# Gates, projections up and mixtures by channel; the second block's input divided by its norm first; GpSimd's elementwise work on VectorE and ScalarE

## The chip, the core and the metric

The kernel runs on one core of one Trainium2 chip. The metric is the device time of one launch in microseconds (us). Three runs of the kernel before took 1385.99, 1386.69 and 1391.58 us; the median is 1386.69.

## The reference

512 tokens of width 1024 in fp32 pass through two blocks. `@` is a matrix product.

```
# first block
h     = rms_norm(x, norm_mix_g)
parts = h @ w_in                     # q, k, v of two attentions, small gates, g_a, g_b (1024 each)
out_a = fox_attention(...)  @ w_fox_up      # 8 heads, forget gates; 512 -> 1024
out_b = nsa_attention(...)  @ w_nsa_up      # 8 heads: compressed, selected, windowed keys; 512 -> 1024
mix   = sigmoid(g_a) * out_a + sigmoid(g_b) * out_b
x     = x + mix @ w_out
x     = x + hierarchical_moe(rms_norm(x, norm_ffn_g))     # 16 experts, 2 per token

# second block
u      = rmsnorm(x, g_pre)
proj   = u @ w_in_2                  # feat_a, z_a, c_q, c_kv, k_pe, z_b, gate logits (2048)
y_a    = rwkv7_branch(feat_a, z_a, ...)                   # ends with @ w_out_a
y_b    = mla_branch(c_q, c_kv, k_pe, z_b, ...)            # ends with @ w_out_b
gates  = sigmoid(gate_logits + b_gate)
merged = gates[:, :1024] * y_a + gates[:, 1024:] * y_b
out    = x + rmsnorm(merged @ w_o, g_post)
```

## The kernel before

Every large product is taken in three passes over split numbers (`mm3`, L118 to L120: high part by high part, low by high, high by low). A weight piece comes from DRAM as `raw`, ScalarE rounds it to `wh` (L109), VectorE subtracts to get `wl` (L112).

`linear_steps` (L128) gives a projection as a list of steps. 128 tokens are stationary and a piece of weight columns moves: with 256 columns a projection with 1024 rows of weight is 4 token tiles x 8 k x 3 matmuls of 128x256, and the result has tokens on the partitions. `Fill` (L291) puts such steps into TensorE's in-order stream between the products of the attention: `pull(t)` lets out steps worth t, each with a price of `3 * n / 2400` us, and `until(None)` lets out what is left. TensorE's stream is written out by hand in this way; on the other engines the scheduler orders the instructions.

First block, 0 to 550 us. q, k, v are projected, then come the heads of the two attentions with gates and projections up as fill (50 to 442 us). The norm's factor r of a token (`c.r`) is not in `hh`, `hl`; a gate applies it as the per-partition scale of its tanh (`tanh_to_dram`, and `gated` in `up`), since tokens are on the partitions there. The gates go to DRAM as `gd`, the gated first branch as `md` (`up`, L713). `twice`/`scaled` (L338) multiply q or k by their head norm on GpSimd, whose squares (L534) are on GpSimd too, and GpSimd adds the heads of the second attention into `ob` (L990). Then `merge` (L181) turns `ob` (L175), projects it with `w_nsa_up` in two halves of 512 columns, reads `gd` and `md`, forms `g = (g + 1) * product` (L201), `mix = mix + g` (L202), and turns `mix` on TensorE (`pt<-ident,mix`, L196) into `mh`, `ml` for `w_out`.

Experts run from 550 to 846 us. The second block begins at 846 us: `turned` (L214) adds the experts' part to x (L1454), multiplies by the gain (`xg`, L227), turns `xg` into `uh`, `ul` (L237), and projects the 416 columns of c_q, c_kv, k_pe. The squares are summed beside it (L241), r comes after the last product, `zc` is scaled by r on ScalarE (L2132), and `rr` is a row of r for each token, repeated over the partitions.

Then the second attention (`mla`, to 1012 us), the recurrence: `shifted` (L1584) projects 128 channels with tokens in the columns, multiplies by `rr` (L1590, VectorE) and shifts; `prepare` and `pairs` (1012 to 1150 us) make decays (`sw`, `C`), `GL`, `GR`, and `H` (L1689, GpSimd); an inversion (1150 to 1192 us), small products, a chain over 8 chunks (1230 to 1309 us). Gates of the second block are fill in these stages: `(product * r + bias)` on VectorE (L2176, L2218), tanh on ScalarE, `(tanh + 1) * product` (L2223). The same `merge` closes it, with `w_out_a` (1309 to 1339 us), then `w_o`, the last norm, and the sum with x.

Of the kernel before, what the change touches and what calls it, by code (L numbers as in the profile page):

```python
# [21 lines left out]
S = 512  # L22
# [18 lines left out]
class Ctx:  # L41
# [108 lines left out]
    def tanh_to_dram(self, pool, dst):  # L150

        def emit(i, ps):
            sg = pool.tile([128, 512], FT, name="sg", bufs=2)
            n = ps.shape[1]
            self.nc.scalar.activation(sg[:, :n], ps, AF.Tanh, scale=self.rh[:, i:i + 1])
            self.nc.sync.dma_start(dst(i), sg[:, :n])
        return emit

    def silu2_to_dram(self, pool, dst, scale=lambda i: 0.5):

        def emit(i, ps):
            sg = pool.tile([128, 512], FT, name="sg", bufs=2)
# [51 lines left out]
    def turned(self, x, get, gain, xgs, scr, hi, lo, steps, first=0):  # L214
# [5 lines left out]
        ms = self.sm.tile([128, NT], FT, name="ms")  # L220
        for _, f in loads[:first]:
            f()
        get(0)
        grow = gain()
        for i in range(NT):
            xg = xgs[i % 2]
            nc.vector.tensor_mul(xg, x[i], grow)  # L227
            if i == 0:
                for _, f in loads[first:]:
                    f()  # L230
            if i + 1 < NT:
                get(i + 1)
# [96 lines left out]
class Attention:  # L329
# [197 lines left out]
def _head_norm(c, z, w, name, scr_pool):  # L527
# [11 lines left out]
def first_mixer(c, I, at, hh, hl):  # L539
# [148 lines left out]
    gd = c.dram.tile([S, D], FT, name="gd")  # L688

    def gate(c0):  # L690
        return c.linear_steps(hh, hl, w_in, 3872 + c0, 256, c.tanh_to_dram(at, lambda i: gd[
            128 * i:128 * i + 128, c0:c0 + 256]))
    md = c.dram.tile([S, D], FT, name="md")
# [8 lines left out]
    def up(c0):  # L702

        m = []

        def gated(i, ps):
            if i % 2 == 0:
                m.append(at.tile([128, 2, 256], FT, name="sg", bufs=2))
            nc.scalar.activation(m[i // 2][:, i % 2], ps, AF.Tanh, scale=c.rh[:, i:i + 1])

        def emit(i, ps):
            v = m[i // 2][:, i % 2]
            nc.vector.scalar_tensor_tensor(v, v, 1.0, ps, op0=OP.add, op1=OP.mult)  # L713
            nc.scalar.dma_start(md[128 * i:128 * i + 128, c0:c0 + 256], v)
        return {f"a{c0}": c.linear_steps(hh, hl, w_in, 2848 + c0, 256, gated),
                f"u{c0}": c.linear_steps(lambda: ot, None, I["w_fox_up"][0], c0, 256, emit)}
# [11 lines left out]
    def second():  # L728
# [4 lines left out]
            ("gn_bias", I["gn_bias_2"], 0), ("g_q", I["g_q_2"], 0), ("g_kv", I["g_kv_2"], 0),  # L733
        ], "mm")
        late.append(trig(c, I, at))
    jobs |= {f"g{c0}": gate(c0) for c0 in range(0, D - 256, 256)}
# [38 lines left out]
    with tc.manual_schedule(engines={mybir.EngineType.PE}):  # L775
# [9 lines left out]
    mix = [at.tile([128, 2, D], FT, name="mix", tag=t, bufs=1) for t in ("t0", "t1")]
    mh, ml = (c.hp.tile([128, 8, S], FR, name=n, tag="f16", bufs=2) for n in ("mh", "ml"))
    ot = at.tile([128, 4, S], FR, name="obh", tag="kv", bufs=1), [
        at.tile([128, S], FR, name="obl", tag=t, bufs=n) for t, n in (("p", 3), ("p", 3), ("p", 3), ("cb", 2))]
    c.token_T(N.ob, *ot)
    c.merge(at, "q", 8, lambda: ot, I["w_nsa_up"][0], gd, md, mix, mh, ml)  # L790
# [55 lines left out]
class Nsa:  # L846
# [99 lines left out]
    def jobs(self, A, out):  # L946
# [14 lines left out]
        def job(h, b):  # L961
# [12 lines left out]
            def prep():  # L974
                if r == 0:
                    self.K[b] = A.keys(two["k"], c.cv["nsa_k"])
                if b == 0:
                    al[h] = at.tile([128, S], FT, name="cb", bufs=2)
                    nc.gpsimd.tensor_scalar(al[h], self.alibi, self.slopes[h], None, op0=OP.mult)
                return A.passes(self.Q[h], self.K[b]), lambda i: al[h][:, 384 - 128 * i:], False  # L980

            def done(pv, rb, ri):
                if r + g + b == 0:
                    self.ob = out()
                    nc.gpsimd.memset(self.ob, 0.0)
# [8 lines left out]
    def compressed(self, g):  # L994
# [14 lines left out]
        def softmax():  # L1009
# [12 lines left out]
            nc.gpsimd.tensor_sub(t, t, m[:, :, :, None].to_broadcast([128, NT, 4, 32]))  # L1022
# [15 lines left out]
        def values(i):  # L1038
# [8 lines left out]
            nc.gpsimd.tensor_add(o, o, tmp)  # L1047
# [26 lines left out]
def route(c, I, mh, ml, x2d, td, xp, keep):  # L1074
# [1228 lines left out]
```

## Time and profile before

| | |
|---|---|
| median of three runs | 1386.69 us |
| profiled execution | 1392.48 us, span of its instructions 1390.7 us |
| granted TensorE clock, mean | 0.960 of 2.4 GHz |
| busy TensorE / VectorE / ScalarE / GpSimd | 1277.1 / 974.8 / 755.6 / 259.3 us |
| chain of work that ended last | TensorE 65%, VectorE 17%, ScalarE 7%, DMA 6% |

A row of a timeline reads: start, length, engine, line, operation, out<-in, shapes, count, and in brackets how long the engine stood idle before it and what released it. Ends of matmuls are modelled, so the pitch of a stream is read from its starts. A group's row ends with busy time, mean length in ns of one, and the idle time before.

### The profile page before, as it was taken

Reading aid. Unit: us, or ns where it says so; the run is one execution under the profiler, and the core shown is the slowest. Engines: PE = TensorE matmul, PEld = TensorE weight load, DVE = VectorE, ACT = ScalarE, POOL = GpSimd, SP = SyncE. Lnnn points to the kernel's source line nnn. Section 1 sums busy time; section 2 is a strip of 40 time slices with the busy share of each in tenths; the row PEclk is TensorE's granted clock in tenths of the full one; section 3 lists DMA queues with packets and bytes.
Section 4 is the critical chain, followed back from the end, with each engine's and each line's share of the span. In section 5 each row is a group of like instructions: output and inputs, shape, how many; then the busy total and the mean of one; then the engine's idle time right before and its main releaser. Section 6 shows DMA issues by size and latency. Waiting matters only on the chain.

```text
span 1390.7 us, 24478 instructions
## 1 busy us (share of the span) xinstructions
PE 1277.1 (92%) x9240; PEld 1082.6 (78%) x9240; DVE 974.8 (70%) x2030; ACT 755.6 (54%) x1291; POOL 259.3 (19%) x226
## 2 busy tenths in 40 slices
PE   7999989988999995999999998999999999799997
PEld 6889978977898774677777776888977667788875
DVE  5664687666665646999999997767668769445555
ACT  5544565654544322788888885655557664233431
POOL 1111032211220002154444421000011012001000
PEclk9999989999999997999999998999999999799999
DMA  6332312222133497999999996541152334233543
GB/s 201 110 122 78 99 54 67 74 68 67 57 121 122 138 323 271 341 369 361 353 346 342 349 313 196 158 138 45 32 163 80 104 109 137 65 114 112 173 138 122
DMA packets 161294, 230.68 MB, mean 166 GB/s; under 512 B 21786, under 2 KB 97869, under 8 KB 161168
## 3 DMA queue, kind: packets, MB, share of 16 engines
q1 hardware_dynamic: 149760, 205.18, 45.1%
q0 software_dynamic: 6224, 18.62, 4.8%
q10 hardware_dynamic: 5184, 5.25, 1.1%
q8 instruction: 74, 1.21, 0.4%
q14 instruction: 52, 0.43, 0.1%
HBM read 200.63 MB, written 30.36 MB: 166 GB/s over the span
## 4 chain that ended last, share of the span: by engine, by line
PE 65%; DVE 17%; ACT 7%; DMA 6%; issue 4%; SPq 2%; POOL 0%; DVEq 0%; POOLq 0%; ACTq 0%
PE mm L118 14%; PE mm L119 14%; PE mm L120 14%; DMA raw<-in_w_in 3%; PE s L461 3%; DVE wl L112 3%; PE s L118 2%; PE s L119 2%; PE s L120 2%; PE pt L488 2%; ACT wh L109 1%; DVE itmp L1779 1%; PE x L118 1%; PE pt L1304 1%; DVE s L475 1%
## 5 line engine op out<-in xcount | busy, mean ns | idle before, releaser
L92 DVE TENSOR_TENSOR wl<-rawe,wh 128x1024 fp32r<-128x1024 f32 x192 | 224.7, 1218 | 23.7 <-ACT wh L90 23.6
L109 ACT ACTIVATE wh<-raw 128x512 fp32r<-128x512 f32 x214 | 131.7, 628 | 120.2 <-PE mm L120 42.5
L118 PE MATMUL mm<-wh,hh 128*128 128x256 f32 (+1 forms) x616 | 183.5, 298 | 12.5 <-ACT wh L109 3.3
L112 DVE TENSOR_TENSOR wl<-raw,wh 128x512 fp32r<-128x512 f32 x214 | 147.5, 702 | 63.7 <-ACT wh L109 58.5
L90 ACT ACTIVATE wh<-rawe 128x1024 fp32r<-128x1024 f32 x192 | 190.8, 1054 | 1.5 <-PE mm L120 1.5
L119 PE MATMUL mm<-wl,hh 128*128 128x256 f32 (+1 forms) x616 | 176.8, 287 | 0.1
L120 PE MATMUL mm<-wh,hl 128*128 128x256 f32 (+1 forms) x616 | 176.7, 287 | 0.2
L118 PEld LDWEIGHTS mm<-wh,hh 128*128 128x128 f32 (+1 forms) x616 | 119.1, 193 | 16.6 <-ACT wh L109 3.5
L119 PEld LDWEIGHTS mm<-wl,hh 128*128 128x128 f32 (+1 forms) x616 | 119.1, 193 | 1.8 <-DVE wl L112 0.4
L120 PEld LDWEIGHTS mm<-wh,hl 128*128 128x128 f32 (+1 forms) x616 | 118.9, 193 | 1.2 <-DVE hl L92 0.7
L1275 POOL DMA_INDIRECT xe<-td,slf x16 | 97.9, 6117 | 116.1 <-issue 73.4
L118 PE MATMUL mm<-wh,uh 128*128 128x256 f32 (+1 forms) x352 | 109.1, 310 | 5.2 <-DVE sg L2218 3.1
L479 ACT ACTIVATE p<-s,m 128x128 f32<-128x128 f32 (+3 forms) x128 | 67.3, 526 | 77.4 <-DVE m L475 54.6
L118 PE MATMUL mm<-wh,xh 128*96 128x512 f32 x256 | 103.5, 404 | 1.2 <-ACT xh L90 1.2
L119 PE MATMUL mm<-wl,uh 128*128 128x256 f32 (+1 forms) x352 | 103.7, 295 | 0.0
L120 PE MATMUL mm<-wh,ul 128*128 128x256 f32 (+1 forms) x352 | 103.4, 294 | 0.0
L120 PE MATMUL mm<-wh,xl 128*96 128x512 f32 x256 | 102.0, 398 | 0.4 <-DVE xl L92 0.4
L119 PE MATMUL mm<-wl,xh 128*96 128x512 f32 x256 | 101.1, 395 | 0.0
L492 DVE SCALAR_TENSOR_TENSOR pl<-pt,ph 128x384 f16<-128x384 f32 (+1 forms) x96 | 57.5, 599 | 32.2 <-ACT ph L491 31.6
L118 PEld LDWEIGHTS mm<-wh,uh 128*128 128x128 f32 x352 | 69.1, 196 | 7.9 <-DVE sg L2218 3.3
L119 PEld LDWEIGHTS mm<-wl,uh 128*128 128x128 f32 x352 | 69.3, 197 | 0.7
L120 PEld LDWEIGHTS mm<-wh,ul 128*128 128x128 f32 x352 | 69.2, 196 | 0.1
(718 smaller groups left out, 3287.0 us busy)
## 6 DMA issues: line engine op xcount, KB each, us to landing
raw<-in_w_in SPq DMA_DIRECT2D x71, 512.0 KB, 4.0
rawe<-in_w_gate SPq DMA_DIRECT2D x64, 512.0 KB, 12.1
rawe<-in_w_down SPq DMA_DIRECT2D x63, 512.0 KB, 11.1
rawe<-in_w_up SPq DMA_DIRECT2D x62, 512.0 KB, 12.5
gd<-sg SPq DMA_DIRECT2D x32, 128.0 KB, 1.9
g<-gd SPq DMA_DIRECT2D x16, 256.0 KB, 4.2
md<-sg ACTq DMA_DIRECT2D x32, 128.0 KB, 2.9
mix<-md SPq DMA_DIRECT2D x16, 256.0 KB, 3.3
```

Of the source, the lines that this page charges most:

```text
L90: nc.scalar.activation(hi, src, AF.Copy, scale=scale)
L92: nc.vector.tensor_sub(lo, src, hi.bitcast(FT))
L109: nc.scalar.activation(wh, raw[:, k:k + m], AF.Copy)
L112: e.tensor_sub(wl, raw[:, k:k + m], wh.bitcast(FT))
L118: nc.tensor.matmul(out, xh, wh, start=start, stop=False)
L119: nc.tensor.matmul(out, xh, wl, start=False, stop=False)
L120: nc.tensor.matmul(out, xl, wh, start=False, stop=stop)
L461: mm = nc.tensor.matmul(si, q[:, 128 * i:w], k[:, :w], start=a == 0, stop=a == len(passes) - 1)
L479: nc.scalar.activation(p[:, o:o + w], si, AF.Exp, bias=m, scale=-1.0)
L488: nc.tensor.transpose(pt[:, j:j + 128], p[:, j:j + 128], c.ident)
L492: nc.vector.scalar_tensor_tensor(pl[:, :w], pt[:, :w], PSC, ph[:, :w], op0=OP.mult, op1=OP.subtract)
L1275: nc.gpsimd.indirect_dma_start(out=xe, out_offset=None, in_=td, in_offset=bass.IndirectOffsetOnAxis(ap=of, axis=0))
```

## The change

Three things change.

By channel. Gates, projections up (`w_fox_up`, `w_out_b_2`) and the mixtures (`w_nsa_up`, `w_out_a_2`) use `channel_steps`: 128 columns of weight are stationary, all 512 tokens move, 24 matmuls of 128x512 where 48 of 128x256 stood (K of 1024), and the result has channels on the partitions. `gd` and `md` are stored as [channel, token]. The mixture is then already the way that `w_out` wants it, and its turning falls out. A gate of the first block now has to be multiplied by a row of r (`opened`), since r belongs to the columns.

Divided first. `turned` of the second block computes r of a token tile before it turns it, and puts r into `xg`. All later factors r go: `zc`, `rr`, `mm<-mm,rr`, `zs`, the gates' `rx`, `c.rh`. The gates' bias moves into the tanh as a per-partition vector.

GpSimd. The elementwise instructions move: `two`, the sums into `ob`, `sw`, `H`, `st`, `o * z`, and two smaller ones to VectorE; the squares and `cb` to ScalarE; the addition of `bv` is part of the gain's instruction.

```diff
+    def channel_steps(self, xh, xl, w, c0, n, emit):
...
+        def product(a, k):
+            if k == 0:
+                bank[0] = self.bank("mm", [128, S])
...
+            self.mm3(bank[0], *(x[:, 128 * a:128 * a + 128] for x in ws[k]), h, l, k == 0, k == K // 128 - 1)
+            if k == K // 128 - 1:
+                emit(c0 // 128 + a, bank[0])
...
+                [(0.64, lambda a=a, k=k: product(a, k)) for a in range(n // 128) for k in range(K // 128)])
+    def merge_channels(self, room, x, w, gd, md, mh, ml):
...
+            def emit(a, ps, g=g, m=m):
+                nc.vector.scalar_tensor_tensor(g[a], g[a], 1.0, ps, op0=OP.add, op1=OP.mult)
+                nc.vector.tensor_add(m[a], m[a], g[a])
+                self.split(mh[:, a], ml[:, a], m[a], 0.5)
...
 # turned
+        def ready(i):
+            get(i)
+            ms = self.sm.tile([128, 1], FT, name="ms")
+            nc.scalar.activation(scr, x[i], AF.Square, accum_out=ms)
+            r = self.rsqrt(ms, [128, 1], 1.0 / D, 1e-6, f"rx{i}")
+            nc.vector.scalar_tensor_tensor(xgs[i % 2], x[i], r, grow, op0=OP.mult, op1=OP.mult)
...
+        ready(0)
+        ready(1)
+        for _, f in loads[first:]:
+            f()
+        for i in range(NT):
+            turn(i)
+            if i + 2 < NT:
+                ready(i + 2)
             for _, f in products[8 * i - 8:8 * i] if i else ():
                 f()
-            nc.scalar.activation(scr, x[i], AF.Square, accum_out=ms[:, i:i + 1])
...
-        self.c.nc.gpsimd.tensor_mul(two, src, r[:, :, :, None].to_broadcast([128, NT, 2, 64]))
+        self.c.nc.vector.tensor_mul(two, src, r[:, :, :, None].to_broadcast([128, NT, 2, 64]))
...
-        nc.gpsimd.tensor_mul(sq[:, :w], z[:, i, :w], z[:, i, :w])
+        nc.scalar.activation(sq[:, :w], z[:, i, :w], AF.Square)
...
 # gates of the first block
+    def opened(ps):
+        sg = at.tile([128, S], FT, name="sg", bufs=2)
+        nc.vector.tensor_mul(sg, ps, row[0])
+        nc.scalar.activation(sg, sg, AF.Tanh, scale=0.5)
+        return sg
...
+        def emit(a, ps):
+            nc.vector.scalar_tensor_tensor(m[a], m[a], 1.0, ps, op0=OP.add, op1=OP.mult)
+            nc.scalar.dma_start(md[128 * a:128 * a + 128], m[a])
...
+        c.token_T(N.ob, *ot2)
         fill.until(None)
...
-    c.token_T(N.ob, *ot)
-    c.merge(at, "q", 8, lambda: ot, I["w_nsa_up"][0], gd, md, mix, mh, ml)
+    c.merge_channels(lambda: at.tile([128, S], FT, name="mg", tag="q", bufs=8), ot2, I["w_nsa_up"][0], gd, md, mh, ml)
...
-                nc.gpsimd.tensor_scalar(al[h], self.alibi, self.slopes[h], None, op0=OP.mult)
+                nc.scalar.activation(al[h], self.alibi, AF.Copy, scale=self.slopes[h])
...
+                if g + b == 0:
+                    nc.vector.tensor_mul(o, pv, rb)
+                else:
+                    tmp = at.tile([128, NT, 64], FT, name="tmp", bufs=2)
+                    nc.vector.tensor_mul(tmp, pv, rb)
+                    nc.vector.tensor_add(o, o, tmp)
...
 # Rwkv
-        nc.vector.tensor_mul(ps, ps, self.rr)
...
-        nc.gpsimd.tensor_sub(sw, C, sw)
+        nc.vector.tensor_sub(sw, C, sw)
...
-        nc.gpsimd.tensor_mul(self.H, GL, self.PC[:, p, :, None, None].to_broadcast([128, NC, 2, CH]))
+        nc.vector.tensor_mul(self.H, GL, self.PC[:, p, :, None, None].to_broadcast([128, NC, 2, CH]))
...
-            nc.vector.tensor_scalar(y[:, p], y[:, p], c.cv["gn_gain"][:, pc], c.cv["gn_bias"][:, pc],
-                                    op0=OP.mult, op1=OP.add)
-            nc.gpsimd.tensor_add(y[:, p], y[:, p], self.bv[p][:, ts])
+            nc.vector.scalar_tensor_tensor(y[:, p], y[:, p], c.cv["gn_gain"][:, pc], self.bv[p][:, ts],
+                                           op0=OP.mult, op1=OP.add)
...
 # second block
-        for i in range(NT):
-            nc.scalar.activation(zc[:, i], zc[:, i], AF.Copy, scale=c.r[:, i:i + 1])
-        rr = c2.tile([128, S], FT, name="rr")
-        c.r_row(rr)
...
-            nc.vector.scalar_tensor_tensor(sg[:, :256], ps, c.r[:, i:i + 1], brs[c0], op0=OP.mult, op1=OP.add)
-            nc.scalar.activation(sg[:, :256], sg[:, :256], AF.Tanh, scale=0.5)
...
+    def opened(a, ps):
+        sg = c2.tile([128, S], FT, name="sg", bufs=4)
+        nc.scalar.activation(sg, ps, AF.Tanh, scale=0.5, bias=c.cv["b_gate"][:, a:a + 1])
+        return sg
```

How the order moves at three places. First TensorE at the end of the first mixer. Before, the last products of the fill (`oah` is the turned first attention) come first, then `ob` (the second attention's result) is turned, and its projection follows:

```order
L118 MATMUL mm<-wh,oah 128x256
L119 MATMUL mm<-wl,oah 128x256
L120 MATMUL mm<-wh,oah 128x256
L175 MATMUL mm<-ident,ob 128x128 x16
L118 MATMUL mm<-wh,obh 128x512
L119 MATMUL mm<-wl,obh 128x512
L120 MATMUL mm<-wh,obl 128x512
```

Now `ob` is turned right behind the last head's product with v (`pv`), and the fill stands between that and the projection:

```order
L545 MATMUL pv<-sh,pl 128x65
L203 MATMUL mm<-ident,ob 128x128 x16
L118 MATMUL mm<-hh,wh 128x512
L119 MATMUL mm<-hl,wh 128x512
L120 MATMUL mm<-hh,wl 128x512
```

45 matmuls of 128x512 (21 of a gate, 24 of a projection up) now lie between the turning of `ob` and the 96 of its projection, and the 8 groups of 4 turnings of `mix` between and behind those 96 are gone.

Second, VectorE where the second block begins. Before, a tile's sum with the experts' part (`rawe<-rawe,s`) is followed at once by `xg`:

```order
L1454 TENSOR_TENSOR rawe<-rawe,s 128x512 x2
L227 TENSOR_TENSOR xg<-rawe 128x1024
L1454 TENSOR_TENSOR rawe<-rawe,s 128x512 x2
L112 TENSOR_TENSOR wl<-rawe,wh 128x416 x2
L92 TENSOR_TENSOR ul<-pt,uh 128x4x128 x2
L227 TENSOR_TENSOR xg<-rawe 128x1024
```

Now the reciprocal root (`rs_t`, `rs_h`, `rs_a`, `rx_y`) of a tile of 128 tokens comes between; the second tile's is mixed in:

```order
L1498 TENSOR_TENSOR rawe<-rawe,s 128x512 x4
L112 TENSOR_TENSOR wl<-rawe,wh 128x416 x2
L73 TENSOR_SCALAR rs_t<-ms 128x1
L74 TENSOR_SCALAR rs_h<-rs_t 128x1
L76 TENSOR_SCALAR rx_y<-rs_t 128x1
L77 TENSOR_SCALAR rx_y<-rx_y 128x1
L80 SCALAR_TENSOR_TENSOR rs_a<-rx_y,rs_h 128x1
L84 SCALAR_TENSOR_TENSOR rx_y<-rs_a,rx_y 128x1
L80 SCALAR_TENSOR_TENSOR rs_a<-rx_y,rs_h 128x1
L73 TENSOR_SCALAR rs_t<-ms 128x1
L84 SCALAR_TENSOR_TENSOR rx_y<-rs_a,rx_y 128x1
L74 TENSOR_SCALAR rs_h<-rs_t 128x1
```

The first `xg` stands 7 rows behind these, and both tiles' sums stand ahead of it.

Third, VectorE in the pairs of the recurrence (`f_r`, `f_v` are shifted features). Before:

```order
L112 TENSOR_TENSOR wl<-raw,wh 128x512
L1682 SCALAR_TENSOR_TENSOR kr<-av,kr 128x512
L1590 TENSOR_TENSOR mm<-mm,rr 128x512
L1683 SCALAR_TENSOR_TENSOR GL<-kr,iP 128x8x64
L1685 TENSOR_SCALAR av<-av,ka_13697,ka_13695 128x512
L1593 SCALAR_TENSOR_TENSOR f_v<-mm,cvec,f_v 128x511
```

Now the product's multiplication by `rr` is gone, and `H` stands in this queue:

```order
L1729 TENSOR_TENSOR av<-f_k,av 128x512
L112 TENSOR_TENSOR wl<-raw,wh 128x512
L1730 TENSOR_TENSOR GL<-av,iP 128x8x64
L1738 SCALAR_TENSOR_TENSOR f_r<-f_r,cvec,av 128x512
L1732 TENSOR_TENSOR H<-GL,PC 128x1024
L1636 SCALAR_TENSOR_TENSOR f_k<-mm,cvec,f_k 128x511
```

13 such multiplications leave VectorE's queue, 4 `H` and 4 `sw` come into it.

## Rows read from the trace of the kernel before

**Rows 1.** The page's busy times and the shares of the chain of work that ended last.

```profile
PE 1277.1 (92%) x9240; PEld 1082.6 (78%) x9240; DVE 974.8 (70%) x2030; ACT 755.6 (54%) x1291; POOL 259.3 (19%) x226
...
PE 65%; DVE 17%; ACT 7%; DMA 6%; issue 4%; SPq 2%; POOL 0%; DVEq 0%; POOLq 0%; ACTq 0%
```

**Rows 2.** Busy time by stage: stretch and its length, then busy us (and instructions) of TensorE, its weight loads, VectorE, ScalarE, GpSimd, granted clock, DMA share, GB/s.

```profile
150.00:230.00 80.00, 70.85 (x646) 65.82 (x645) 61.75 (x189) 46.41 (x88) 22.66 (x45) 0.94 0.23 66
230.00:300.00 70.00, 65.04 (x653) 61.30 (x653) 45.33 (x116) 41.06 (x84) 14.94 (x14) 1.00 0.26 76
300.00:442.00 142.00, 129.04 (x1237) 121.41 (x1234) 90.16 (x255) 68.81 (x137) 25.27 (x28) 0.98 0.27 85
442.00:482.00 40.00, 35.68 (x161) 28.74 (x161) 25.00 (x52) 11.76 (x21) 0.76 (x4) 0.91 0.38 122
...
1050.00:1150.00 100.00, 90.59 (x557) 68.75 (x556) 72.28 (x121) 64.25 (x122) 13.04 (x9) 0.95 0.33 99
1150.00:1192.00 42.00, 33.52 (x211) 29.87 (x209) 40.15 (x93) 15.15 (x29) 6.50 (x5) 1.00 0.45 134
```

**Rows 3.** Timeline of TensorE at 1013 us, where a stream of 128x512 gives way to one of 128x256 at full clock: the first and the last start of each, 11 steps apart.

```profile
1011.15 0.39 PE L119 MATMUL mm<-ul,wh 128*128 128x512 f32 x1
...
1013.65 0.28 PE L118 MATMUL mm<-wh,uh 128*128 128x256 f32 x1
...
1014.96 0.28 PE L120 MATMUL mm<-wh,ul 128*128 128x256 f32 x1
```

**Rows 4.** Timeline of TensorE over the first merge.

```profile
440.76 1.33 PE L175 MATMUL mm<-ident,ob 128*128 128x128 f32 x8
443.71 0.63 PE L175 MATMUL mm<-ident,ob 128*128 128x128 f32 x4 [1.61 <-DVE obl L179]
...
446.04 0.77 PE L118 MATMUL mm<-wh,obh 128*128 128x512 f32 x1 [0.91 <-DVE obl L179]
446.60 0.63 PE L119 MATMUL mm<-wl,obh 128*128 128x512 f32 x1
...
451.72 0.56 PE L119 MATMUL mm<-wl,obh 128*128 128x512 f32 x1
...
476.11 0.63 PE L196 MATMUL pt<-ident,mix 128*128 128x128 f32 x4 [1.64 <-DVE mix L202]
476.49 0.47 PE L118 MATMUL mm<-wh,mh 128*128 128x512 f32 x1
```

**Rows 5.** Chain of waits of the second merge (start, length, what): one turning of four blocks, then from 1322 us what it waited for.

```profile
1315.59 0.44 PE pt L196 x4
...
1322.76 4.03 DMA g<-gd
1326.79 0.69 DVE wl L112
1327.49 3.93 DMA raw<-in_w_o
```

**Rows 6.** Groups of GpSimd, shapes kept apart.

```profile
L338 POOL TENSOR_TENSOR two<-zk,rk_y 128x512 f32<-128x512 f32 x8 | 8.6, 1070 | 59.7 <-PE x L349 58.2 <-DVE q L92 1.5
...
L1689 POOL TENSOR_TENSOR H<-GL,PC 128x1024 f32<-128x1024 f32 x4 | 8.0, 2007 | 78.4 <-DVE GL L1687 78.4
```

**Rows 7.** Groups of VectorE, shapes kept apart: two that go, and four whose lengths price what comes.

```profile
L202 DVE TENSOR_TENSOR mix<-mix,g 128x512 f32<-128x512 f32 x16 | 11.1, 691 | 0.4
...
L1590 DVE TENSOR_TENSOR mm<-mm,rr 128x512 f32<-128x512 f32 x13 | 9.0, 694 | 4.4 <-PE mm L120 4.4
...
L2218 DVE SCALAR_TENSOR_TENSOR sg<-mm,rx_y,br 128x256 f32<-128x256 f32 x16 | 7.7, 482 | 17.1 <-PE mm L120 16.8
...
L989 DVE TENSOR_TENSOR tmp<-pv,ri 128x256 f32<-128x256 f32 x16 | 6.8, 422 | 0.9
...
L1694 DVE TENSOR_TENSOR GR<-f_r,P 128x512 f32<-128x512 f32 x4 | 5.4, 1360 | 0.0
...
L80 DVE SCALAR_TENSOR_TENSOR rs_a<-rf_y,rs_h 128x1 f32<-128x1 f32 x18 | 4.0, 220 | 0.6
```

**Rows 8.** Timeline of VectorE: the same two operations, alone and beside GpSimd.

```profile
1028.59 0.43 DVE L1580 TENSOR_SCALAR sw<-sw 128x512 f32<-128x512 f32 x1 [0.47 <-ACT sw L1578]
...
1030.99 1.52 DVE L1580 TENSOR_SCALAR sw<-sw 128x512 f32<-128x512 f32 x1
...
1032.51 1.21 DVE L1652 TENSOR_TENSOR_SCAN C<-reset,sw 128x512 f32<-128x512 f32 x1
...
1054.77 2.33 DVE L1652 TENSOR_TENSOR_SCAN C<-reset,sw 128x512 f32<-128x512 f32 x1
```

**Rows 9.** Timeline of GpSimd at those times.

```profile
1030.66 1.56 POOL L1653 TENSOR_TENSOR sw<-C,sw 128x512 f32<-128x512 f32 x1 [20.44 <-DVE C L1652]
...
1053.67 2.34 POOL L1689 TENSOR_TENSOR H<-GL,PC 128x1024 f32<-128x1024 f32 x1 [18.22 <-DVE GL L1687]
```

**Rows 10.** Chain of waits in the recurrence's pairs.

```profile
1049.40 0.61 DVE mm L1590
...
1053.67 2.35 POOL H L1689
```

**Rows 11.** Chain of waits where the second block begins.

```profile
858.42 1.94 PE pt L237 x8
...
877.86 0.65 ACT zc L2132
```

More of the change, by code (lines that the diff above doesn't have):

```diff
@@ L219, in turned, with turn @@
         loads, products = steps
-        ms = self.sm.tile([128, NT], FT, name="ms")
         for _, f in loads[:first]:
             f()
-        get(0)
         grow = gain()
-        for i in range(NT):
[L226 to L232, printed above, removed]
+        def ready(i):
[4 more added lines that the diff above has]
+            nc.vector.scalar_tensor_tensor(xgs[i % 2], x[i], r, grow, op0=OP.mult, op1=OP.mult)
+        def turn(i):
             ts = slice(128 * i, 128 * i + 128)
@@ L685, in fox, with over @@
         return (scale, queries, prep), lambda: (*fx["v"][:2], h), done
-    gd = c.dram.tile([S, D], FT, name="gd")
+    gd = c.dram.tile([D, S], FT, name="gd")
+    row = []
+    def over():
+        row.append(at.tile([128, S], FT, name="t", bufs=2))
+        c.r_row(row[0], "mm")
+    def opened(ps):
[3 more added lines that the diff above has]
+        return sg
     def gate(c0):
-        return c.linear_steps(hh, hl, w_in, 3872 + c0, 256, c.tanh_to_dram(at, lambda i: gd[
-            128 * i:128 * i + 128, c0:c0 + 256]))
-    md = c.dram.tile([S, D], FT, name="md")
+        return c.channel_steps(hh, hl, w_in[:, 3872:], c0, 256, lambda a, ps: nc.sync.dma_start(
+            gd[128 * a:128 * a + 128], opened(ps)))
+    md = c.dram.tile([D, S], FT, name="md")
     ot = []
@@ L702, in up @@
     def up(c0):
[L704 to L716, printed above, removed]
+        m = {}
+        def emit(a, ps):
+            nc.vector.scalar_tensor_tensor(m[a], m[a], 1.0, ps, op0=OP.add, op1=OP.mult)
+            nc.scalar.dma_start(md[128 * a:128 * a + 128], m[a])
+        return {f"a{c0}": c.channel_steps(hh, hl, w_in[:, 2848:], c0, 256, lambda a, ps: m.update({a: opened(ps)})),
+                f"u{c0}": c.channel_steps(lambda: ot, None, I["w_fox_up"][0], c0, 256, emit)}
     jobs = {}
@@ L732, in second @@
             ("k_a", I["k_a_2"], 0), ("r_k", I["r_k_2"].rearrange("a b -> (a b)"), 0), ("gn_gain", I["gn_gain_2"], 0),
-            ("gn_bias", I["gn_bias_2"], 0), ("g_q", I["g_q_2"], 0), ("g_kv", I["g_kv_2"], 0),
+            ("gn_bias", I["gn_bias_2"], 0), ("g_q", I["g_q_2"], 0), ("g_kv", I["g_kv_2"], 0), ("b_gate", I["b_gate_2"], 0),
         ], "mm")
+        nc.vector.tensor_scalar(c.cv["b_gate"], c.cv["b_gate"], 0.5, None, op0=OP.mult)
         late.append(trig(c, I, at))
+    jobs["row"] = ([], [(0.4, over)])
     jobs |= {f"g{c0}": gate(c0) for c0 in range(0, D - 256, 256)}
@@ L781, in first_mixer @@
               [(43 + 2 * n, f) for n, f in enumerate(comp)])
+        ot2 = at.tile([128, 4, S], FR, name="obh", tag="t0", bufs=1), [
+            at.tile([128, S], FR, name="obl", tag=t, bufs=n) for t, n in (("p", 3), ("p", 3), ("p", 3), ("cb", 2))]
+        c.token_T(N.ob, *ot2)
         fill.until(None)
[L785 removed]
     mh, ml = (c.hp.tile([128, 8, S], FR, name=n, tag="f16", bufs=2) for n in ("mh", "ml"))
[L787 to L790 removed]
+    c.merge_channels(lambda: at.tile([128, S], FT, name="mg", tag="q", bufs=8), ot2, I["w_nsa_up"][0], gd, md, mh, ml)
     return mh, ml
@@ L1962, in trig @@
     nc.scalar.activation(small[:, 5:7], small[:, 5:7], AF.Sin)
-    cs = pool.tile([128, NT, 128], FT, name="t", bufs=2)
+    cs = pool.tile([128, NT, 128], FT, name="sg", bufs=2)
     nc.gpsimd.memset(cs, 0.0)
@@ L2138, in second_block @@
     zbd = c.dram.tile([S, 512], FT, name="zbd")
-    gd = c.dram.tile([S, D], FT, name="gd2")
-    md = c.dram.tile([S, D], FT, name="md2")
+    gd = c.dram.tile([D, S], FT, name="gd2")
+    md = c.dram.tile([D, S], FT, name="md2")
     od = c.dram.tile([S, 512], FT, name="od")
@@ L2244, in second_block @@
     with tc.tile_pool(name="fin", bufs=1, reuse_waits="tile") as fin:
-        mix = [fin.tile([128, 2, D], FT, name="mix", bufs=2) for _ in range(2)]
         mh, ml_ = (fin.tile([128, 8, S], FR, name=n) for n in ("mh", "ml"))
-        c.merge(fin, "g", 4, lambda: (yt[:, 0], yt[:, 1]), I["w_out_a_2"], gd, md, mix, mh, ml_)
+        c.merge_channels(lambda: fin.tile([128, S], FT, name="mg", bufs=8), (yt[:, 0], yt[:, 1]), I["w_out_a_2"], gd, md, mh, ml_)
         grow = fin.tile([128, D], FT, name="grow2")
```

96 lines of the change are left out of this document (42 added, 54 removed).

## The prediction

> **What bounds the kernel now.** I read the page's busy times first, then its chain of work, then busy times by stage, then timelines of the stages that the change touches. TensorE is busy 92% of the span and holds 65% of the chain; VectorE follows with 70% and 17%; GpSimd is busy 19% and holds 0% of the chain [rows 1]. So a matmul saved is mostly time saved, and an instruction that leaves GpSimd saves nothing by itself: what matters is what it does to VectorE, where most of it lands. By stages [rows 2] TensorE is full in the first mixer except at 150 to 230 us, where VectorE is busy 61.75 of 80 us; and in the inversion (1150 to 1192) VectorE is the bound with 40.15 of 42.
>
> **Columns.** Each block's gates and projections up issue 2 x 384 + 192 = 960 matmuls of 128x256 now (4 jobs of 96 for each of two gates, 4 of 48 for the projection); they become 480 of 128x512. In one unbroken stream the starts of 128x512 lie (1013.65 - 1011.15) / 11 = 0.2273 us apart, those of 128x256 (1014.96 - 1013.65) / 11 = 0.1191 [rows 3]. A pair costs 0.2382, so 960 mergers save 960 x 0.0109 = 10.5 us. They are fill or stand in bare streams, so I put all of it on the path; what the fill then no longer covers is priced with the first mixer below. The Trainium skill, "TensorE: Matmul & The Clock Gate", section "Back-to-back issue gap", gives the gap of an isolated matmul as its columns over 2.4 GHz plus 2.5 ns, which would put the fixed part of a matmul at 2.5 ns and this term at an estimated 960 x 2.5 ns = 2.4 us; rows 3 show four times that.
>
> **First merge.** From the first turning of `ob` to the first product with `w_out` it takes 476.49 - 440.76 = 35.7 us [rows 4]. What must stay is 96 x 0.2273 = 21.8 and 16 turnings at 0.11 (0.44 for four [rows 5]) = 1.8. The rest: waits of 1.61, 0.91 and 1.64 = 4.2; 12 steps at (451.72 - 446.60) / 12 = 0.427, the lower of the two clock levels, granted after these waits, 12 x 0.2 = 2.4 too long; 8 groups of turnings of `mix` x 0.44 = 3.5 [rows 4, 5]. With 45 matmuls between the turning of `ob` and its use (45 x 0.2273 = 10.2 us) the split of `ob` is covered and the engine comes into the 96 running; the turnings are gone. That is 10.1. New is that `ob` is turned right behind the last head: reciprocal, gate, product and sum on VectorE, two of them at 0.42 [rows 7], some 2 us in which the fill now lies behind the waiting instruction and can't help. Per channel tile VectorE has three instructions of 0.6 to 0.69 and one for the next weights, 2.5 us against 12 x 0.2273 = 2.7 on TensorE, so it nearly fills up. I take 8 gained; between 4 and 10.
>
> **Second merge.** The same 3.5 us of turnings go, but here the chain runs through `g<-gd` (4.03) and the first weights of `w_o` (3.93) [rows 5], which the change doesn't shorten, and VectorE then works off what is late without a gap. I take 3; between 0 and 6.
>
> **Divided first, the recurrence.** 13 multiplications by `rr` x 0.694 = 9.0 us leave VectorE [rows 7]. Of the 13 about nine are links of the chain between a product and its shift, like the one at 1049.40 [rows 10]: 9 x 0.61 = 5.5. `H` is on the chain once with 2.35 us; on VectorE it should cost what `GR` costs, 1.36 [rows 7], but all four and four `sw` x 0.69 now queue with the work that sets the pace, 8.2 us added to 72.28 of 100 [rows 2]. Net I take 3 gained; between 3 lost (all of the new on the path, two thirds of the old off it) and 7 gained.
>
> **Inversion.** Of the 16 `sg` x 0.482 = 7.7 us of L2218 [rows 7] four lie in the stage that VectorE bounds: 2 gained.
>
> **GpSimd gone.** An operation that takes 0.43 us on VectorE took 1.52 beside `sw` on GpSimd, one of 1.21 took 2.33 beside `H` [rows 8, 9]. VectorE was stretched in this way, by over 80 ns, sixteen times, 10 us in all, always beside an elementwise instruction of GpSimd; these two are the largest but for one. About a third of it is on the path: 3 gained; between 0 and 8.
>
> **Start of the second block.** Before, `xg` waits for no norm. Now a square on ScalarE and nine or ten instructions of some 0.2 us [rows 7] come first, for two tiles woven into each other, and tile 1's `xg` must be ready before the first product. TensorE is idle or at half clock there already (eight turnings take 1.94 us at 858.42 [rows 11]), so it is late by what the two norms add, less the weights' own arrival: 2 lost; between 0 and 5. The scaling of `zc` [rows 11] is gone behind the products, where TensorE had other work: 0.
>
> **First mixer, VectorE.** Added: `two` 20 x 0.69 = 13.8, sums into `ob` 20 x 0.42 = 8.4, rows of r 16 x 0.69 = 11.0, small ones 1.4, less 1.2 for the gating in wider pieces: 33 us [rows 7], on 197 of 292 us between 150 and 442 [rows 2]. `two` falls mostly into 150 to 230, where with a few rows of r some 17 us meet 18 of idle time. GpSimd took 1.07 for a `two` [rows 6], so a single head's chain gets shorter by 0.4 and its queue longer. TensorE waits 27 us in these 292 now. Nothing in the trace shows the same heads with a fuller VectorE, so the bounds are 5 gained (the shorter steps win) and 33 lost (all on the path). I take 6 lost, near the lower end, since from 230 us on VectorE has a third of the time free.
>
> **Sum.** -10.5 - 8 - 3 - 3 - 2 - 3 + 2 + 6 = -21.5. Against the profiled execution, 1392.48, that gives 1371; against the median of the three runs shown, 5.8 below it, 1365. I forecast 1367.
>
> **Rivals.**
> - VectorE becomes the bound of the first mixer. The multiplication of a gate's product by the row of r, `two` and the sums queue between the row maxima and the low halves of p; TensorE waits for p while its product banks stay full. For it: 150 to 230 us. Against it: the other two stages. At the full 33 us in place of 6 the time is 1367 + 27 = 1394, slower; the change is a loss from about 26 us on.
> - The saved columns come back as waits. Where heads set the pace (maximum, exponential, turning), less fill only means more idle time: the 10.5 of the columns are lost but for 2, and the first mixer costs 11: 1367 + 8.5 + 5 = 1380.5. For it: TensorE's 27 us of waiting there. Against it: 45 matmuls of fill are left over behind the last head, so the fill doesn't run dry.
> - Matmuls of 128x256 are no dearer per column when they run in the fill than the wide ones: the term falls to 2 or 3 us, 1375. The rule named above is this case. Against it: rows 3.
> - More is gained: TensorE is granted less than full speed at 150 to 230 (0.94) and 442 to 482 (0.91) [rows 2], each time behind waits, and with fewer stretched instructions these recover too, the terms come in at their better ends: 1352.
>
> **How the numbers follow.** Forecast 0.50 (own range 1358 to 1377), VectorE as the bound 0.10, columns given back 0.20, no gain by width 0.05, more 0.15. About 0.5%, 7 us, is what a measurement can tell from no change: below 1379.8 is faster, above 1393.6 slower. Faster: 0.49 of the forecast, 0.08 of columns given back, 0.04 of no gain by width, 0.15 of more = 0.76. Slower: 0.06 of VectorE as the bound and 0.01 of the rest = 0.07. Same 0.17. The range goes from the larger gain to just beyond the columns given back: 1350 to 1386.
>
> **What would show it.** Right: 128x512 starts 0.227 to 0.23 apart in gates and projections up; no `pt<-ident,mix`; between the last fill product of the first mixer and the first product with `w_out` 96 unbroken starts, 22 to 24 us; no stretched VectorE instruction; the inversion 2 us shorter. Wrong: TensorE waiting for `two`, `q` or a gate's `sg` on VectorE by over 10 us more at 150 to 442 (VectorE as the bound); the first mixer as long as before, 392 us from 50 us to the end of its fill (columns given back); the first product of the second block over 5 us later behind the experts than before.

## The result, and the profile after

The changed kernel takes 1368.83 us (median of four runs, 1366.22 to 1371.63) against 1388.4 before, measured in four runs: ratio 0.9856, 95% interval 0.9828 to 0.9884. The forecast was 1367. The profiled execution took 1371.63, its span is 1369.8, 20.9 us below the 1390.7 of before.

The page's busy times and PEclk row of the changed kernel, to be held against [rows 1]:

```profile
span 1369.8 us, 22178 instructions
PE 1259.4 (92%) x8216; PEld 1008.3 (74%) x8216; DVE 979.0 (71%) x2071; ACT 762.0 (56%) x1285; POOL 150.2 (11%) x117
PEclk9999999999999997899999998899999999789999
```

TensorE has 1024 recorded matmuls fewer and stays at 92%. VectorE gained 41 instructions, yet its busy time rose by 4.2 us only, where the prediction's own rows (33 and 8.2 that come, 9.0 and 2 x 7.7 that go) leave 17. That is the first sign that its old instructions became shorter.

The table gives the time between starts of named matmuls in the profiled executions. A stage with the same code in several kernels scatters (the start from 161.2 to 166.4, the first mixer from 258.95 to 261.7, the first merge from 43.1 to 44.0, the way from `w_out` to the experts from 80.1 to 84.6, the pairs from 132.9 to 137.0; the inversion only from 42.29 to 42.32), so a single difference under 3 us says little in most of them.

| from ... to | before | after | change |
|---|---|---|---|
| start to first score of a head | 163.8 | 165.8 | +1.9 |
| to the last head's product with v | 266.5 | 258.9 | -7.6 |
| to the first product with `w_out` (first merge) | 46.2 | 43.1 | -3.0 |
| to the first expert product | 80.2 | 83.6 | +3.5 |
| to the last expert product of the first two weights | 277.0 | 277.2 | +0.2 |
| to the first product of the second block | 26.4 | 33.3 | +6.9 |
| to the turning of k_pe (`kr`) | 25.0 | 23.1 | -1.9 |
| to the last head of the second attention | 123.2 | 119.5 | -3.8 |
| to the last `GR`,`GL` product (prepare, pairs) | 137.0 | 135.1 | -1.9 |
| to the first `Tr`,`A` product (inversion) | 48.4 | 42.3 | -6.0 |
| to the first product of the second merge | 115.6 | 110.5 | -5.1 |
| to its last | 25.6 | 22.1 | -3.5 |
| to the end | 55.8 | 55.3 | -0.5 |

The total is that of the forecast, the places are partly others. TensorE's timeline in the first merge, the answer to [rows 4]:

```profile
424.82 0.55 PE L203 MATMUL mm<-ident,ob 128*128 128x128 f32 x3
426.29 0.33 PE L203 MATMUL mm<-ident,ob 128*128 128x128 f32 x1 [0.92 <-DVE ob L1035]
428.31 0.63 PE L203 MATMUL mm<-ident,ob 128*128 128x128 f32 x4 [1.70 <-DVE obl L207]
430.64 1.08 PE L203 MATMUL mm<-ident,ob 128*128 128x128 f32 x4 [1.70 <-DVE obl L207]
433.42 1.09 PE L203 MATMUL mm<-ident,ob 128*128 128x128 f32 x4 [1.70 <-DVE obl L207]
434.16 0.78 PE L118 MATMUL mm<-hh,wh 128*128 128x512 f32 x1
...
436.87 0.46 PE L118 MATMUL mm<-hh,wh 128*128 128x512 f32 x1
437.16 0.39 PE L119 MATMUL mm<-hl,wh 128*128 128x512 f32 x1
...
440.11 0.39 PE L120 MATMUL mm<-hh,wl 128*128 128x512 f32 x1
```

The turnings run one group at a time: each waits 1.70 us until the group before has been split (`obl`). Products and turnings share two banks (`bank("mm")`), and here one belongs to a gate's product that the fill left half done, whose last 21 matmuls are the ones from 434.16 on. So the sixteen turnings take 9.3 us, and then TensorE is at the lower clock level (steps of 0.43 us from 434.73) until 436.87. At the full level 13 steps from 437.16 to 440.11 are 0.227 us each, the same as in [rows 3].

The second block's start, ScalarE first, then VectorE:

```profile
848.37 0.99 ACT L109 ACTIVATE wh<-rawe 128x416 fp32r<-128x416 f32 x2 [5.46 <-DMA rawe<-in_w_in]
849.27 1.04 ACT L255 ACTIVATE rawe<-rawe 128x1024 f32<-128x1024 f32 x1
```

```profile
845.61 1.29 DVE L1498 TENSOR_TENSOR rawe<-rawe,s 128x512 f32<-128x512 f32 x2 [1.68 <-DMA rawe<-x2d]
...
850.43 0.15 DVE L73 TENSOR_SCALAR rs_t<-ms 128x1 f32<-128x1 f32 x1 [0.28 <-ACT rawe L255]
...
852.88 1.28 DVE L257 SCALAR_TENSOR_TENSOR xg<-rawe,rx_y 128x1024 f32<-128x1024 f32 x1
...
855.54 1.28 DVE L257 SCALAR_TENSOR_TENSOR xg<-rawe,rx_y 128x1024 f32<-128x1024 f32 x1
```

Tile 0's sum is done at 846.9, its square begins 2.4 us later, behind two weight roundings that waited for their DMA, the root takes from 850.43 to 852.88, and the second `xg` comes 2.7 us behind the first.

### The profile page after: what moved, and what is told of

It is laid out like the page before. It is cut to its first block, busy times and chain, and to the rows that moved or that the text cites. A ratio compares the mean times of both kernels' runs of the same rounds, so it can differ in the third digit from the quotient of the medians.

```text
span 1369.8 us, 22178 instructions
## 1 busy us (share of the span) xinstructions
PE 1259.4 (92%) x8216; PEld 1008.3 (74%) x8216; DVE 979.0 (71%) x2071; ACT 762.0 (56%) x1285; POOL 150.2 (11%) x117
## 4 chain that ended last, share of the span: by engine, by line
PE 40%; DVE 6%; ACT 5%; DMA 5%; issue 4%; DVEq 0%; SPq 0%; ACTq 0%; POOL 0%; POOLq 0%
PE mm L118 9%; PE mm L119 8%; PE mm L120 8%; DMA x2d<-y,slt 2%; PE s L120 2%; PE s L118 2%; PE s L119 2%; DMA raw<-in_w_in 1%; PE s L495 1%; DVE wl L112 1%; DMA raw<-in_w_o 1%; ACT wh L109 1%; PE pt L522 1%; PE pt L1348 1%; PE pt L1948 1%
## 5 line engine op out<-in xcount | busy, mean ns | idle before, releaser
L118 PE MATMUL mm<-wh,hh 128*128 128x256 f32 (+1 forms) x360 | 106.3, 295 | 6.6 <-ACT hh L90 3.3
L118 PE MATMUL mm<-uh,wh 128*128 128x512 f32 x264 | 110.4, 418 | 0.8 <-ACT sg L2207 0.8
L119 PE MATMUL mm<-ul,wh 128*128 128x512 f32 x264 | 105.7, 401 | 0.0
L120 PE MATMUL mm<-uh,wl 128*128 128x512 f32 x264 | 105.5, 400 | 0.0
L120 PE MATMUL mm<-wh,hl 128*128 128x256 f32 (+1 forms) x360 | 104.5, 290 | 0.1
L119 PE MATMUL mm<-wl,hh 128*128 128x256 f32 (+1 forms) x360 | 104.4, 290 | 0.1
L118 PEld LDWEIGHTS mm<-wh,hh 128*128 128x128 f32 (+1 forms) x360 | 70.2, 195 | 8.1 <-ACT hh L90 3.7
L119 PEld LDWEIGHTS mm<-wl,hh 128*128 128x128 f32 (+1 forms) x360 | 70.2, 195 | 1.1 <-DVE wl L112 0.4
L525 ACT ACTIVATE ph<-pt 128x384 f16<-128x384 f32 (+1 forms) x96 | 50.2, 522 | 29.6 <-PE pt L522 29.0
L509 DVE CUSTOM_DVE_ANT_0 s<-s,cb 128x128 f32<-128x128 f32 (+1 forms) x96 | 47.4, 496 | 20.9 <-ACT p L513 10.1
L118 PEld LDWEIGHTS mm<-uh,wh 128*128 128x128 f32 x264 | 50.7, 192 | 11.8 <-ACT sg L2207 1.2
```

Source lines behind the costliest of these rows:

```text
L118: nc.tensor.matmul(out, xh, wh, start=start, stop=False)
L119: nc.tensor.matmul(out, xh, wl, start=False, stop=False)
L120: nc.tensor.matmul(out, xl, wh, start=False, stop=stop)
L509: nc.vector.tensor_tensor_reduce(out=si, in0=si, in1=bias(i), scale=1.0, scalar=3e38, op0=OP.add, op1=OP.min, accum_out=m)
L525: nc.scalar.activation(ph[:, :w], pt[:, :w], AF.Copy, scale=PSC)
```

## The experiments

Each is the changed kernel with one edit. Ratios are to the kernel before on the same chip; the changed kernel's is 0.9856.

**Columns undone.**

```diff
+            half, k = divmod(j, K // 128)
+            ts = slice(256 * half, 256 * half + 256)
-            self.mm3(bank[0], *(x[:, 128 * a:128 * a + 128] for x in ws[k]), h, l, ...)
+            self.mm3(bank[0][:, ts], *(x[:, 128 * a:128 * a + 128] for x in ws[k]), h[:, ts], l[:, ts], ...)
```

> The changed kernel with every product by channel issued as two halves of 256 tokens, one after the other into the same bank: 960 matmuls of 128x512 become 1920 of 128x256 again, nothing else moves. Theory (the pitch of a matmul has a fixed part, and the saved time is on the path): starts 0.119 apart in place of 0.227 to 0.23, 960 x 0.0109 = 10.5 us slower than the changed kernel, 1379. Rival (saved columns come back as waits): the pitch is the same but the time only 0 to 4 us more, 1369 to 1373, with shorter waits of TensorE in the first mixer. Rival (nothing to gain by width beyond 2.5 ns a matmul): pitch 0.1145, 2 to 3 us more, 1371.

Ratio 0.9939 (0.9921 to 0.9956). The difference to 0.9856 is 0.0083 of 1388.4, 11.5 us. In its timeline of TensorE:

```profile
442.54 0.28 PE L120 MATMUL mm<-hh,wl 128*128 128x256 f32 x1
...
444.32 0.28 PE L120 MATMUL mm<-hh,wl 128*128 128x256 f32 x1
```

15 steps of 0.1187, two of them 0.2373 against 0.227 for one wide matmul. The run splits 1152 matmuls and not 960 (its trace has 9368 for 8216): the 192 of the two mixtures, which were wide in the kernel before too, come from the same function. So the 11.5 us, uncertain by 4.6, belong to 1152; 960 of them make an estimated 9.6, and by the pitch, 960 x (0.2373 - 0.227), 9.9. The first mixer takes 267.5 us (266.5 before, 258.9 after), the second attention 2.3 more than after. The theory holds; both rivals fall.

**GpSimd's elementwise work given back.** `two`, the squares, `cb`, the sums into `ob`, `sw`, `H`, `st` and `o*z` are issued on GpSimd again:

```diff
-        self.c.nc.vector.tensor_mul(two, src, r[:, :, :, None].to_broadcast([128, NT, 2, 64]))
+        self.c.nc.gpsimd.tensor_mul(two, src, r[:, :, :, None].to_broadcast([128, NT, 2, 64]))
```

> The changed kernel with two, the squares, cb, the sums into ob, sw, H, st and o*z given back to GpSimd. Theory (the terms of the sum: 3 us of stretching and 1 of H come back, 4 us of the fuller VectorE in the first mixer go): within 2 us of the changed kernel, 1367 to 1371, the mixer from first score to last head 3 to 4 shorter, pairs 3 to 4 longer. Rival (the fuller VectorE costs the first mixer more than it seems): 4 or more faster, under 1365. Rival (stretching and the longer steps of GpSimd cost more than I put): 6 or more slower, over 1375, with VectorE instructions over 80 ns too long in the trace again.

Ratio 0.9868 (0.9828 to 0.9907): no difference that can be told, as the theory has it for the whole. The busy times of its first mixer, from first score to last head (stretch and its length, TensorE, its loads, VectorE, ScalarE, GpSimd), and then those of the changed kernel:

```profile
163.80:423.60 259.80, 235.41 (x1901) 190.46 (x1900) 191.11 (x547) 141.10 (x272) 61.20 (x84) 0.98 0.24 73
```

```profile
165.75:424.70 258.95, 235.47 (x1902) 190.59 (x1900) 203.30 (x584) 149.53 (x292) 4.04 (x23) 0.98 0.24 73
```

With 12 us less on VectorE the mixer is no shorter. The shorter mixer and longer pairs that the theory named were not seen. VectorE is stretched again: 22 of its instructions are over 80 ns longer than the same ones of the changed kernel, by 14.7 us in all, 10 of them in this mixer, and none of that can be told in the time. None of the 22 lies in the inversion, which takes 42.3 us as in the changed kernel.

**No norm ahead of the second block.**

```diff
-            nc.scalar.activation(scr, x[i], AF.Square, accum_out=ms)
-            r = self.rsqrt(ms, [128, 1], 1.0 / D, 1e-6, f"rx{i}")
-            nc.vector.scalar_tensor_tensor(xgs[i % 2], x[i], r, grow, op0=OP.mult, op1=OP.mult)
+            nc.vector.tensor_mul(xgs[i % 2], x[i], grow)
```

> The changed kernel without the norm of the second block's input: no squares, no reciprocal root, xg is x times the gain. This leaves the division by the norm out. Theory (the norm ahead of the first turning is what makes the start of the second block 6.9 us longer): last expert product to first product of the second block 26 to 28 us in place of 33.3, the whole 4 to 5 us faster, 1364. Rival (the two sums ahead of xg, or the weights, are what is late): over 30 us in place of 33.3, under 2 us faster.

Ratio 0.9806 (0.9766 to 0.9846). The first product comes 27.9 us behind the last expert product, `kr` 51.8 (51.4 before, 56.4 after). So the norm ahead of the turning costs 4.6 us net of the 5.0 by which `kr` came later, as the theory has it.

**VectorE's multiplications put back.** `nc.vector.tensor_mul(ps, ps, one)` between 13 shifted products and their shifts, and one ahead of each of 16 tanh of a gate.

> The changed kernel with 13 multiplications by one on VectorE between a shifted product and its shift (where the row of r stood), and 16 of a gate's product by one ahead of its tanh. Theory (these instructions were on the path): 3 us in the pairs and 2 to 4 in the inversion, 1374 in all; the stretch from the last GR,GL product to the first Tr,A product grows from 42.3 towards the 48.4 of the kernel before. Rival (the inversion became shorter by the wider columns, not by VectorE): that stretch stays at 42 to 43, under 2 us in all.

Ratio 0.9843 (0.9798 to 0.9888): no loss that can be told. Pairs took 133.3 us (135.1 after), the inversion 43.4 (42.3), with two of the gates' products, 1.4 us, in it. 20 us of VectorE work in the second block, the 13 products ahead of the shifts among it, cost 1 us that can be seen. Nor is it the columns that made the inversion shorter: 41.3 in the run with halves. Both theory and rival fall.

**What shortened the inversion.** In the kernel before, GpSimd's four products of `zs` with the row of r lay in that stage. First GpSimd, then VectorE, of the kernel before:

```profile
1156.98 1.30 POOL L2158 TENSOR_TENSOR zs<-zs,rr 128x512 f32<-128x512 f32 x1 [4.33 <-ACT zs L2157]
```

```profile
1156.79 0.29 DVE L1781 TENSOR_TENSOR Ti<-Ti,itmp 128x135 f32<-128x135 f32 x1
1157.12 1.34 DVE L1779 TENSOR_TENSOR itmp<-A,Ti 128x156 f32<-128x156 f32 x1
1158.49 0.32 DVE L1781 TENSOR_TENSOR Ti<-Ti,itmp 128x156 f32<-128x156 f32 x1
```

The same instruction after, of 156 columns, beside nothing on GpSimd:

```profile
1149.02 0.32 DVE L1823 TENSOR_TENSOR itmp<-A,Ti 128x156 f32<-128x156 f32 x1
```

Four instructions were so stretched by 1.0 to 1.1 us each. The run gives GpSimd a product with one there again:

```diff
                 nc.scalar.activation(z, bank[0], AF.Copy)
+                nc.gpsimd.tensor_mul(z, z, one.to_broadcast([128, S]))
```

> The changed kernel with four multiplications of zs by one on GpSimd, where the row of r stood. Theory (in the kernel before each of these four stretched one instruction of VectorE in the inversion by 1.0 to 1.1 us, and VectorE bounds that stage): the stretch from the last GR,GL product to the first Tr,A product 46 to 47 us in place of 42.3, with four VectorE instructions over 1 us long among itmp, Ti and R; the whole 3 to 4 slower, 1372 to 1373. Rival (the inversion became 6 us shorter by the waits for sg on VectorE that fell out): 42 to 43.5, under 1.5 slower.

The stage takes 45.5 us in place of 42.3. Three instructions of that kind and one weight's `wl` are stretched, by 3.26 us together:

```profile
1143.75 1.20 DVE L1823 TENSOR_TENSOR itmp<-A,Ti 128x192 f32<-128x192 f32 x1
...
1150.28 1.13 DVE L1823 TENSOR_TENSOR itmp<-A,Ti 128x240 f32<-128x240 f32 x1
```

The place and nearly the size are as expected, and the rival falls. The whole, 0.9843 (0.9805 to 0.9880), is too scattered to show 3 us. The 6.0 us are accounted for by a sum: 4.2 us of stretching and 1.9 of four `sg` (4 x 0.48) less on VectorE, whose busy time in this stage is 43.6 us in place of 49.8. Put back, 3.26 us of stretching cost 3.2 here, and 1.4 us of `sg` cost 1.1 in the run with the multiplications put back.

**Another bank for the turning of `ob`.**

```diff
-        c.token_T(N.ob, *ot2)
+        c.token_T(N.ob, *ot2, tag="s")
```

> The changed kernel with the four turnings of ob in the two banks that the attention's scores used, in place of the two that products use, of which a half finished gate product holds one. Theory (one free bank makes the four groups run one after the other, 2.3 to 2.8 us each): first to last turning of ob 9.3 us in the changed kernel, 4 to 5 here, no wait of 1.7 us for obl, the first product with w_out 4 to 5 us earlier behind the last head; the whole 3 to 5 faster, 1365. Rival (the split of ob on ScalarE and VectorE, 1.5 us a group, sets the pace whatever the banks): 7 us or more for the turnings, under 2 us faster.

Ratio 0.9787 (0.9739 to 0.9836). TensorE:

```profile
425.42 0.52 PE L203 MATMUL s<-ident,ob 128*128 128x128 f32 x3
426.97 0.77 PE L203 MATMUL s<-ident,ob 128*128 128x128 f32 x5 [1.03 <-DVE ob L1035]
429.00 0.63 PE L203 MATMUL s<-ident,ob 128*128 128x128 f32 x4 [1.26 <-DVE obl L207]
429.79 0.63 PE L203 MATMUL s<-ident,ob 128*128 128x128 f32 x4 [0.16 <-DVE obl L207]
```

Two groups are under way at once, the turnings take some 5 us, and the first merge 37.15 in place of 43.1; the rival falls. Once more, in more rounds:

> ob_bank once more, on the same chip as ob_early and in more rounds. Theory (6 us of the merge are won, the rest of the first 9 was scatter): ratio 0.981 to 0.983. Rival (all of it holds): 0.979 or less.

Ratio 0.9803 (0.9773 to 0.9834), median 1363.8, the merge 37.16 again: between what theory and rival named, nearer to the theory. By the ratios this version is some 7 us faster than the changed kernel, uncertain by about 6; 6 us of it are shown by the stage.

**The second block's start, two tries.** Squares ahead of the roundings, by giving these a scale that comes from the sums of squares:

> The changed kernel with the rounding of the last four weight pieces of the second block's first projection made to wait for the squares of the first two token tiles (their scale is a one that comes from the sums of squares). Theory (the first square stood 2.4 us behind two roundings that waited for their DMA): first turning of xg 2 us earlier behind the last expert product, the first product of the second block 1.5 to 2.5 us earlier (31 in place of 33.3), the whole 1 to 2 faster. Rival (the roundings are then late for the first product): 33 or more, no gain.

Ratio 0.9846 (0.9804 to 0.9889). The first turning came 1.2 us earlier, the second 1.5 us later (VectorE now had four `wl`, a wait of 2.4 us for `uh` and the first tile's `ul` between the two `xg`), the first product 34.6 behind the last expert product. The rival holds. Then four steps of the first product ahead of the second tile's turning:

```diff
             turn(i)
+            for _, f in products[:4] if not i else ():
+                f()
             if i + 2 < NT:
                 ready(i + 2)
```

> The changed kernel with the first four steps of the second block's first product put right behind the turning of the first token tile, ahead of the third tile's sum and the second tile's turning. Theory (TensorE stands behind the second tile's norm and behind sums of later tiles at the lower clock level): first product 3 to 4 us earlier behind the last expert product (30 in place of 33.3), the kr products 2 to 3 us earlier, 1366. Rival (what is late is the second tile, whatever stands ahead of it): the first product is earlier, the kr products within 1 us of before.

Ratio 0.9865 (0.9834 to 0.9896). The first product is 4 us earlier (29.2), `kr` 4.5 us later (60.9 behind the last expert product, 56.4 after): the third tile's sum now stands behind those steps, and TensorE waits 2.7 us for its norm at 871.51. Worse than its rival. Together with the other bank:

> The edits of ob_bank and early together. Theory: both gains, 8 us faster than the changed kernel, 1359 to 1362. Rival: only that of ob_bank, 1363.

Ratio 0.9836 (0.9808 to 0.9863), no better than the bank alone, with the merge at 38.2 us and `kr` as late as in the run before. The theory falls. Likewise the bank with the squares first:

> The edits of ob_bank and sq_first together. Theory: the gains add up, 4 to 7 faster than the changed kernel, 1362 to 1365. Rival (what comes earlier waits for the weights' DMA in the projection with w_out and behind the experts): less than half of the sum.

Ratio 0.9822 (0.9789 to 0.9855), again no better than the bank alone; the theory falls.

**How near VectorE is to being the bound of the first mixer.**

```diff
+        for _ in range(2):
             self.c.nc.vector.tensor_mul(two, src, r[:, :, :, None].to_broadcast([128, NT, 2, 64]))
...
+        for _ in range(2):
             nc.vector.tensor_mul(sg, ps, row[0])
```

> The changed kernel with each of the 20 multiplications into two and the 16 of a gate's product by the row of r issued twice: 25 us more of VectorE work in the first mixer, nothing else. Theory (VectorE has room there, its load was priced too high): from first score to last head 259 to 264, under 3 us more in all, 1369 to 1372. Rival (VectorE is close to being the bound, as a rival of the prediction had it): 8 us or more, over 1377, with longer waits of TensorE for q and for p.

Ratio 0.9929 (0.9903 to 0.9954), 10 us slower, the mixer 274.8 us in place of 258.9. TensorE's waits in it, of the changed kernel first:

```profile
PE x L383 <- DVE q L396: 5.8, 4, 2.7
...
PE mm L118 <- DVE sg L732: 2.8, 3, 1.6
```

```profile
PE mm L118 <- DVE sg L734: 6.4, 4, 2.6
PE x L384 <- DVE q L397: 6.0, 4, 2.9
...
PE mm L2020 <- DVE sg L734: 2.1, 1, 2.1
```

The rival holds by the time, but not by the waits that it named: those for `q` stay at 6 us. The waits that grew are those for a product's bank (`sg`): from 2.8 to 6.4 us, and from 1.0 to 2.1 for a second group. That is 4.7 of the 15.8 us by which the mixer is longer. The stretch's granted clock also fell from 0.98 to 0.94. Whether it is VectorE's load or the longer way of each product and each `two` (both instructions stand one behind the other) this run doesn't tell apart.

## Why the prediction was right, and where its steps were not

- **Columns**, 10.5 forecast: about 9.6, as the share of 960 in what the run with halves lost. The Trainium skill, "TensorE: Matmul & The Clock Gate", section "Back-to-back issue gap", gives an isolated matmul 2.5 ns beyond its columns, by which the term would be an estimated 2.4 us. The runs show 0.2373 us for two narrow ones against 0.227 for a wide one, 10.3 ns, and disagree.
- **First merge**, 8 forecast, 3.0 measured. The step that failed is that with 45 matmuls behind the turning of `ob` "the split of `ob` is covered". They cover the split of the last group; the turnings themselves wait for it, since a half finished product holds the second bank. The run with another bank gives back 6.0, and with it the merge gains 9.0, near the forecast. That the turnings of `mix` go, and that the 96 run unbroken, was right (445.85 to 467.82 is 22.0 us).
- **Second merge**, 3 forecast, 3.5 measured. No run takes it back.
- **Recurrence**, 3 forecast, 1.9 measured, which is within the scatter of the pairs, and with the multiplications put back the stage is no longer. So "about nine are links of the chain" did not mean that it shortens by them; what is late next there is not shown. The price of `H` was wrong too: `GR`'s 1.36 was stretched by `H` on GpSimd itself; after, `GR` takes 0.69 and `H` 1.22.
- **Inversion**, 2, and **GpSimd gone**, 3 forecast; 6.0 measured in the inversion alone. The stretching was mis-sized: I compared instructions with others of their shape, and those of the inversion each have a shape of their own. Paired with the same instruction after, 27 of VectorE's were 19.2 us too long in the kernel before, all beside GpSimd, and 4.2 us of that lay where VectorE was the bound.
- **Start of the second block**, 2 lost forecast; 5.0 at `kr`, 4.6 by the run without the norm. The square behind two roundings was not foreseen, but putting it first didn't help; by the two tries, the second tile's `xg` and the later tiles' sums are late next.
- **First mixer, VectorE**, 6 lost forecast; about 1, less than the scatter: with columns undone it takes 267.5 against 266.5 before, and giving 12 us back to GpSimd made no difference. The margin behind it is small, as the run with 25 us more shows.

The sum of the measured terms (-9.6 - 3 - 3.5 - 2 - 6 + 5 + 1) is -18.1, against a forecast of -21.5 and 19.6 measured. That the total came so near is in part luck: errors in the first merge and at the second block's start were paid by the first mixer, and a little by the inversion. In no term stands the stage ahead of the second merge (small products and the chain over 8 chunks), 5.1 us shorter; with columns undone 2.0 of it come back, and the cause of the rest stays open. The start and the way to the experts came out 1.9 and 3.5 us longer, within their scatter.

Of the signs that the prediction named, those for being right came: starts 0.227 us apart, no turning of `mix`, 96 unbroken starts, a shorter inversion, and in the whole trace only two instructions of VectorE over 80 ns longer than the shortest of their kind in any run, by 0.35 us together. Two of those for being wrong came as well. The first product of the second block is 6.9 us later behind the experts, over the 5 named, by the norm. And the fill of the first mixer ends at 445.8 us, no earlier than before (440.8), since the turnings of `ob` now lie ahead of that end. That does not mean that the columns came back as waits: the last head comes 7.6 us sooner behind the first score, and undoing the columns takes that back.

The rivals: columns given back and no gain by width fall with the run of halves. VectorE as the bound did not come about, though 25 us more of it would have taken 10 of the 20 us. The larger gain did not come by the clock: mean granted 0.957, before 0.960.

## What to carry to other kernels

Whoever lets out work of a queue of fill between two steps should ask which banks a product left half done still holds: here that made four groups of turnings wait for each other, 6 us, while 45 matmuls stood ready behind them. What GpSimd does to VectorE is seen only by pairing the same instruction in two traces, and it counts in the stage that VectorE bounds, not by its sum. Work taken off a chain of waits is not time saved until the run that puts it back has shown it.

## What the runs showed of the hardware

An elementwise product on GpSimd of 1.1 to 1.8 us held up one instruction of VectorE at a time by 0.7 to 1.1 us in the inversion (0.32 to 1.34, 0.38 to 1.36), whatever its own length. Others beside it keep theirs. GpSimd, then VectorE, of the kernel before; an `itmp` of 0.38 us and the stretched `Ti` behind it both begin while one product of `zs` runs:

```profile
1163.33 1.79 POOL L2158 TENSOR_TENSOR zs<-zs,rr 128x512 f32<-128x512 f32 x1 [5.05 <-ACT zs L2157]
```

```profile
1163.59 0.38 DVE L1779 TENSOR_TENSOR itmp<-A,Ti 128x220 f32<-128x220 f32 x1
1164.00 1.36 DVE L1781 TENSOR_TENSOR Ti<-Ti,itmp 128x220 f32<-128x220 f32 x1
```

The Trainium skill, "Advanced Engine Details and Errata", section "VectorE Performance Modes", says that VectorE's second port is shared with GpSimd, so that GpSimd's instructions and those of VectorE that use both ports block each other. The runs agree as far as VectorE is held up, and show where that is paid; which of its instructions use both ports no run shows.
